# Streaming 640 tokens as 320 and 320 columns instead of 256 and 384 in the weight-stationary products

## The chip, the core and the metric

The kernel runs on one core of a Trainium2 chip. A core has a matrix engine (TensorE; the profile calls its multiplications PE and its weight loads PEld), a vector engine (DVE), a scalar engine (ACT), a general engine (POOL) and a queue that issues transfers (SP). Each has its own instruction stream, and they meet by semaphores. The metric is the device time of one execution in microseconds (us).

## What is computed

Two layers of a transformer step over 640 tokens, 512 latent tokens and 128 context tokens, with a model width of 1024. Everything is float32. A layer is

```python
h = rms_norm(x, norm_attn) * (1.0 + sc_a) + sh_a
proj = h @ w_in                        # 1024 -> 2304: queries, keys, values
...                                    # two kinds of attention
x = x + g_a * (mix @ w_out)            # 1024 -> 1024
h = rms_norm(x, norm_ffn) * (1.0 + sc_f) + sh_f
gate, up = jnp.split(h @ w_gate_up, 2, axis=-1)     # 1024 -> 2 x 2816
x = x + g_f * ((jax.nn.silu(gate) * up) @ w_down)   # 2816 -> 1024
```

Shift, scale and gate (sh, sc, g) come from a conditioning vector, one for the latent and one for the context tokens; the context tokens stand last, in columns 512 to 639.

## The kernel before

The stream x is kept transposed: eight tiles xT[k] of 128 features by 640 tokens. A float32 product is made of three products of rounded halves: each operand is split into a high half (hi) and a low rest (lo), and `prod` adds hi·hi, hi·lo and lo·hi in PSUM. These are the three matmuls of lines 476, 477 and 478.

There are two kinds of product. In the input projection and the attention, the tokens are the stationary operand. In the output projection (`residual` with w_out), the gate and up products (`ffn`) and the down products (`residual` with w_down), the weights are stationary: a block of 128 by 128 weights is loaded and the 640 tokens stream past it. A matmul here streams at most 512 columns, so the tokens go as two groups, and each weight block is loaded once for each group. The groups are `GROUPS`: columns 0 to 255, and 256 to 639. `acc2` hands out the two accumulators as neighbouring slices of one PSUM tile S (three such tiles are in rotation), laid so that the first group ends where one bank ends, and `columns` cuts the operands. For one output block the first group's products all come before the second's: with eight input blocks that is 24 matmuls of 256 columns and then 24 of 384.

The layer's two norms use the same split. The last three output blocks of a `residual` that stands before a norm are done group by group: all three blocks' first group, then the first group's statistics (line 383 sums squares over features on TensorE, lines 95 to 101 take the reciprocal root on DVE, line 387 spreads it over the partitions on TensorE as `rb`), and `norm_apply` writes columns 0 to 255 of the eight normalised tiles hi[k] and lo[k]; then the same for the second group, columns 256 to 639. Per tile `norm_chunk` scales on DVE (line 403), writes hi on ACT (line 86 or 409) and lo on DVE (line 87) or POOL (line 410). In the norm ahead of the gate and up products, the tiles are called k (hi) and q (lo) in the profile.

The order of each engine's instructions is set when the program is built: a scheduler with a timing model of its own sorts ready work, and an engine then runs its list strictly in that order. Waits follow the overlap of columns, tile by tile: a matmul that reads columns 0 to 255 of hi[k] doesn't wait for a write of columns 256 to 639.

Of the kernel before, what the change touches and what calls it, by code (L numbers as in the profile page):

```python
# [21 lines left out]
KC = D // P  # L22
# [3 lines left out]
NT = SEQ + DEC  # L26
# [6 lines left out]
CT = NTILE - 1  # L33
SPLIT = 256
GROUPS = ((0, SPLIT), (SPLIT, NT))
NKEY = DEC + SEQ + PAST
CTX0 = DEC
OLD0 = DEC + SEQ
# [5 lines left out]
class Net:  # L44
# [25 lines left out]
    def mm(self):  # L70
        return self.ps.tile([P, 512], F32, tag="mm", name="mm", bufs=2)

    def acc2(self):

        s = self.S()[:, SPLIT:SPLIT + NT]
        return s, [s[:, a:b] for a, b in GROUPS]


    def split(self, hi, lo, src, bias=None):
# [310 lines left out]
    def norm_apply(self, state, group, rb):  # L390
        g0, g1 = GROUPS[group]
        for k in range(KC):
            self.norm_chunk(state, k, g0, g1, rb)
# [239 lines left out]
    def stack_keys(self, l, pr, d):  # L633

        nc = self.nc
        ka = self.t([P, NKEY], f"k{2 * pr}", F32R)
        kb = self.t([P, NKEY], f"k{2 * pr + 1}", F32R)
        self.ks[pr] = (ka, kb)
# [3 lines left out]
        for i, src in enumerate(tiles):  # L642
            nc.tensor.transpose(ps[:, i * P:(i + 1) * P], src, self.ident)
        src = ps[:, 0:NKEY]
        nc.scalar.activation(ka[0:64], src[0:64], AF.Copy)
# [266 lines left out]


    def columns(self, w, act, group, order):
        a, b = GROUPS[group]
        return [((w[0][:, k], w[1][:, k]), (act[0][k][:, a:b], act[1][k][:, a:b])) for k in order]

    def add_gated(self, l, which, mb, src, a, b):
# [11 lines left out]
    def residual(self, l, act, which, order, nxt=None, side=(), steps=1):  # L930

        if nxt:
            self.stat_begin()
        for mb in range(KC - 3 if nxt else KC):
            w = self.w_next()
            s, parts = self.acc2()
            for i in range(2):  # L940
                self.prod(parts[i], self.columns(w, act, i, order))
            self.add_gated(l, which, mb, s, 0, NT)
            if nxt:
                self.stat_add(mb, 0, NT)
                if mb == 2:
                    self.warm(AF.Silu if nxt[1] else AF.Exp)
            for _ in range(steps):
                self.step(side)
        if not nxt:
            return None  # L950
        while side:
            self.step(side)
        state = self.norm_begin(*nxt)
        last = [(mb, self.w_next(), self.acc2()[1]) for mb in (KC - 3, KC - 2, KC - 1)]
        for i, (a, b) in enumerate(GROUPS):
            for mb, w, parts in last:
                self.prod(parts[i], self.columns(w, act, i, order))
                self.add_gated(l, which, mb, parts[i], a, b)
                self.stat_add(mb, a, b)
            rb = self.mm()  # L960
            self.norm_stats(rb, range(a // P, b // P))
            self.norm_apply(state, i, rb)
        return state[2]

    def ffn(self, l, h, side):
        nc = self.nc
        nxt = None
        for pi, n in enumerate(PARTS):
            if pi == 2:
                while side:  # L970
                    self.step(side)
            if pi < 2:
                act = [[self.t([P, NT], f"{x}{j}", F32R) for j in range(n)] for x in ("hi", "lo")]
            else:
                v = self.t([P, 6, NT], "V", F32R)
                act = [[self.t([P, NT], "Q", F32R, bufs=6) for _ in range(n)], [v[:, j] for j in range(n)]]
            for j in range(n):
                out = []
                for u in range(2):
                    w = self.w_next()  # L980
                    s, parts = self.acc2()
                    for i in range(2):
                        self.prod(parts[i], self.columns(w, h, i, range(KC)))
                    out.append(s)
                    if u == 0:
                        sg = self.t([P, NT], "P", bufs=3)
                        nc.scalar.activation(sg, s, AF.Silu)
                        if pi or j > SKIP:
                            self.step(side)
                nc.vector.tensor_tensor(sg, out[1], sg, ALU.mult)  # L990
                self.split(act[0][j], act[1][j], sg)
                if pi or j > SKIP:
                    self.step(side)
            if pi == len(PARTS) - 1 and l + 1 < DEPTH:
                nxt = (l + 1, 0)
            r = self.residual(l, act, 5, range(n), nxt, side)
        return r
# [92 lines left out]
```

## Time and profile before

| | us |
|---|---|
| median of 3 runs | 1778.3 (1777.71 to 1779.84) |
| the profiled execution | 1776.35 |
| its span, first to last instruction | 1774.6 |
| TensorE busy with matmuls | 1724.7 (97%) |
| DVE busy | 1014.1 (57%) |
| ACT busy | 615.6 (35%) |

The busy time of TensorE counts the pipeline's overlap, so a matmul's own duration there (0.28 us for 256 columns) is longer than the time until the next one starts; the pace is read from the starts. The granted TensorE clock was 0.989 of full speed on average: 1.00 is 2.4 GHz, and in some short stretches it was 0.5, which is 1.2 GHz.

### The profile page before, as it was taken

What the parts mean: (1) busy time and instruction counts of PE and PEld (TensorE: products, weight loads), DVE (VectorE), ACT (ScalarE), POOL (GpSimd) and SP (SyncE); (2) the same over time, 40 slices, a digit from 0 to 9 for tenths busy, and PEclk for the clock granted to TensorE, in tenths of its full rate; (3) what the DMA queues carried; (4) which work ended last, traced back from release to release, by engine and by line L of the source; (5) the groups of instructions that cost most, each with busy time, mean ns of one, the idle gap of its engine ahead of it and who ended that gap; (6) DMA issues with size and microseconds to landing.
All of it is one profiled execution on the core that took longest, in us unless ns stands there. A gap on an engine that the chain in (4) does not pass through costs nothing.

```text
span 1774.6 us, 29153 instructions
## 1 busy us (share of the span) xinstructions
PE 1724.7 (97%) x12194; PEld 1609.7 (91%) x12194; DVE 1014.1 (57%) x1757; ACT 615.6 (35%) x1143; POOL 277.6 (16%) x266
## 2 busy tenths in 40 slices
PE   8889999999999999999999998999999999999999
PEld 6767978888999999899999997888999999999998
DVE  5765667877577877723247885778463232223222
ACT  4422376732422121212235434767252212221220
POOL 0332634400000000000002354453010000000000
PEclk9999999999999999999999999999999999999999
DMA  9343211153155554412222211112212222121212
GB/s 350 109 154 98 55 25 25 49 182 127 56 187 168 162 201 154 145 70 72 77 82 86 81 34 45 31 40 75 72 48 95 72 72 78 66 96 51 93 54 78
DMA packets 44259, 169.20 MB, mean 95 GB/s; under 512 B 5600, under 2 KB 8416, under 8 KB 32864
## 3 DMA queue, kind: packets, MB, share of 16 engines
q1 hardware_dynamic: 44128, 167.34, 28.5%
q8 instruction: 96, 1.57, 0.4%
q14 instruction: 35, 0.29, 0.1%
HBM read 152.90 MB, written 3.93 MB: 88 GB/s over the span
## 4 chain that ended last, share of the span: by engine, by line
PE 91%; DVE 3%; ACT 3%; DMA 1%; issue 1%; POOL 1%; SPq 0%; DVEq 0%; POOLq 0%; ACTq 0%
PE S L476 23%; PE S L477 23%; PE S L478 23%; PE S L687 3%; PE mm L792 3%; PE S L771 2%; PE S L688 2%; PE mm L327 2%; PE mm L788 2%; PE S L233 2%; PE mm L266 1%; PE mm L476 1%; PE mm L477 1%; PE mm L478 1%; DVE mx L707 1%
## 5 line engine op out<-in xcount | busy, mean ns | idle before, releaser
L83 ACT ACTIVATE whi<-raw 128x1024 fp32r<-128x1024 f32 (+2 forms) x192 | 196.2, 1025 | 811.2 <-PE S L477 734.8
L477 PE MATMUL S<-q,whi 128*128 128x256 f32 (+1 forms) x1408 | 436.3, 310 | 0.0
L478 PE MATMUL S<-k,wlo 128*128 128x256 f32 (+1 forms) x1408 | 434.6, 309 | 0.0
L476 PE MATMUL S<-k,whi 128*128 128x256 f32 (+1 forms) x1408 | 432.5, 310 | 1.5 <-ACT k L86 1.4
L84 DVE TENSOR_TENSOR wlo<-raw,whi 128x1024 fp32r<-128x1024 f32 (+2 forms) x192 | 229.9, 1200 | 183.1 <-ACT whi L83 175.9
L476 PEld LDWEIGHTS S<-k,whi 128*128 128x128 f32 x1408 | 265.5, 189 | 12.4 <-issue 10.1
L477 PEld LDWEIGHTS S<-q,whi 128*128 128x128 f32 x1408 | 266.7, 189 | 4.2 <-issue 4.2
L478 PEld LDWEIGHTS S<-k,wlo 128*128 128x128 f32 x1408 | 266.0, 189 | 2.5 <-issue 2.5
L478 PE MATMUL S<-hi,wlo 128*128 128x384 f32 (+1 forms) x768 | 237.9, 310 | 0.0
L477 PE MATMUL S<-lo,whi 128*128 128x384 f32 (+1 forms) x768 | 237.7, 310 | 0.0
L476 PE MATMUL S<-hi,whi 128*128 128x256 f32 (+1 forms) x768 | 237.7, 311 | 0.0
L923 DVE SCALAR_TENSOR_TENSOR x<-S,modT,x 128x128 f32<-128x128 f32 (+2 forms) x137 | 66.4, 524 | 208.6 <-PE S L478 208.6
L310 DVE SCALAR_TENSOR_TENSOR Q<-V,cT,Q 128x512 f32<-128x512 f32 x224 | 152.3, 743 | 0.0
L476 PE MATMUL S<-whi,hi 128*128 128x256 f32 x512 | 147.6, 288 | 1.9 <-ACT Q L241 1.9
L476 PEld LDWEIGHTS S<-hi,whi 128*128 128x128 f32 x768 | 144.0, 188 | 5.9 <-issue 5.0
L478 PEld LDWEIGHTS S<-hi,wlo 128*128 128x128 f32 x768 | 144.5, 188 | 3.4 <-issue 3.4
L478 PE MATMUL S<-whi,lo 128*128 128x256 f32 x512 | 145.8, 286 | 0.0
L477 PE MATMUL S<-wlo,hi 128*128 128x256 f32 x512 | 145.8, 285 | 0.0
L707 DVE TENSOR_REDUCE mx<-S 128x1 f32<-128x768 f32 x128 | 119.1, 950 | 46.3 <-PE S L688 46.0
L477 PEld LDWEIGHTS S<-lo,whi 128*128 128x128 f32 x768 | 144.4, 188 | 0.8 <-issue 0.8
L990 DVE TENSOR_TENSOR P<-S,P 128x640 f32<-128x640 f32 x44 | 36.2, 823 | 148.1 <-PE S L478 148.1
L476 PEld LDWEIGHTS S<-whi,hi 128*128 128x128 f32 x512 | 97.8, 191 | 8.2 <-issue 3.4
(206 smaller groups left out, 2820.7 us busy)
## 6 DMA issues: line engine op xcount, KB each, us to landing
raw<-in_w_gate_up SPq DMA_DIRECT2D x44, 1024.0 KB, 4.8
V<-in_w_mod SPq DMA_DIRECT2D x64, 512.0 KB, 3.9
raw<-in_w_in SPq DMA_DIRECT2D x16, 1024.0 KB, 4.8
raw<-in_w_down SPq DMA_DIRECT2D x16, 1024.0 KB, 5.0
Q<-in_w_mod SPq DMA_DIRECT2D x32, 256.0 KB, 3.1
raw<-in_w_out SPq DMA_DIRECT2D x8, 1024.0 KB, 5.1
raw<-in_w_down SPq DMA_DIRECT2D x8, 768.0 KB, 4.3
raw<-raw SPq DMA_DIRECT2D x40, 128.0 KB, 2.2
```

What stands on the lines that cost most here:

```text
L83: nc.scalar.activation(hi, src, AF.Copy)
L84: nc.vector.tensor_tensor(lo, src, hi.bitcast(F32), ALU.subtract)
L233: nc.tensor.matmul(o, lhsT=l_[k][:, c], rhs=r_[:, w], start=k == 0 and i == 0, stop=k == KC - 1 and i == 2)
L310: ins = nc.vector.scalar_tensor_tensor(a, v, self.cT[:, k, c:c + 1], a, ALU.mult, ALU.add)
L476: self.nc.tensor.matmul(out, lhsT=lh, rhs=rh, start=(i == 0), stop=False)
L477: self.nc.tensor.matmul(out, lhsT=lh, rhs=rl, start=False, stop=False)
L478: self.nc.tensor.matmul(out, lhsT=ll, rhs=rh, start=False, stop=(i == n - 1))
L687: nc.tensor.matmul(out, lhsT=Q[j][:, cols], rhs=keys[:, k0:k0 + n], start=True, stop=False)
L707: nc.vector.tensor_reduce(mx, s[:, 0:n], AX.X, ALU.max, negate=True)
L792: nc.tensor.matmul(o[64 * j:64 * j + 64], lhsT=self.V[:, v, 512 + 64 * j:576 + 64 * j], rhs=pts[j][:, i * P:(i + 1) * P], start=first, sto ...
L923: self.nc.vector.scalar_tensor_tensor(x[:, s:e], src[:, s - a:e - a], self.m(l, which, mb, c), x[:, s:e], ALU.mult, ALU.add)
L990: nc.vector.tensor_tensor(sg, out[1], sg, ALU.mult)
```

## The change

A second pair of groups, `EVEN`, is added: columns 0 to 319, and 320 to 639. `acc2` takes the groups as an argument, with `EVEN` for a default, and `columns` takes the bounds themselves. All gate and up products and the output blocks of the output and down projections use `EVEN`; the last three output blocks of a `residual` that stands before a norm, and the norm itself, stay with `GROUPS`. No instruction is added or removed: each pair of a 256-column and a 384-column matmul becomes two of 320.

```diff
 GROUPS = ((0, SPLIT), (SPLIT, NT))
+EVEN = ((0, NT // 2), (NT // 2, NT))
...
-    def acc2(self):
-
-        s = self.S()[:, SPLIT:SPLIT + NT]
-        return s, [s[:, a:b] for a, b in GROUPS]
+    def acc2(self, groups=EVEN):
+
+        a = 512 - groups[0][1]
+        s = self.S()[:, a:a + NT]
+        return s, [s[:, a:b] for a, b in groups]
...
     def columns(self, w, act, group, order):
-        a, b = GROUPS[group]
+        a, b = group
...
             s, parts = self.acc2()
-            for i in range(2):
-                self.prod(parts[i], self.columns(w, act, i, order))
+            for part, group in zip(parts, EVEN):
+                self.prod(part, self.columns(w, act, group, order))
...
-        last = [(mb, self.w_next(), self.acc2()[1]) for mb in (KC - 3, KC - 2, KC - 1)]
+        last = [(mb, self.w_next(), self.acc2(GROUPS)[1]) for mb in (KC - 3, KC - 2, KC - 1)]
         for i, (a, b) in enumerate(GROUPS):
             for mb, w, parts in last:
-                self.prod(parts[i], self.columns(w, act, i, order))
+                self.prod(parts[i], self.columns(w, act, (a, b), order))
...
                     s, parts = self.acc2()
-                    for i in range(2):
-                        self.prod(parts[i], self.columns(w, h, i, range(KC)))
+                    for part, group in zip(parts, EVEN):
+                        self.prod(part, self.columns(w, h, group, range(KC)))
```

The scheduler, with the same rules, lays TensorE's list out anew. DVE's and ACT's lists differ in a few neighbouring swaps far from any norm; POOL's and SP's are the same. The lines of the changed kernel that follow the two new lines are numbered two higher (476 to 478 become 478 to 480, 383 becomes 385, 387 becomes 389).

On TensorE, where the second layer's output projection ends and its gate products begin (hi_ and lo_ are the attention's output, k_ and q_ the normalised tiles, the low halves wlo and whi the weights), the list before reads

```order
L478 MATMUL S<-hi_10853,wlo 128x384
L387 MATMUL mm<-ident,rstd 128x128 x2
L476 MATMUL S<-k_12972,whi 128x256 x3
L383 MATMUL mm<-ones,PT 128x1 x3
L477 MATMUL S<-q_12980,whi 128x256
L478 MATMUL S<-k_12972,wlo 128x256
L476 MATMUL S<-k_12973,whi 128x256
```

and, some 30 products further, where the second group's reciprocal roots are spread,

```order
L477 MATMUL S<-q_12986,whi 128x256
L478 MATMUL S<-k_12978,wlo 128x256
L476 MATMUL S<-k_12979,whi 128x256
L387 MATMUL mm<-ident,rstd 128x128 x3
L477 MATMUL S<-q_12987,whi 128x256
L478 MATMUL S<-k_12979,wlo 128x256
```

The list of the changed kernel at the same place:

```order
L480 MATMUL S<-hi_10853,wlo 128x384
L389 MATMUL mm<-ident,rstd 128x128 x2
L385 MATMUL mm<-ones,PT 128x1 x3
L389 MATMUL mm<-ident,rstd 128x128 x3
L478 MATMUL S<-k_12972,whi 128x320 x3
L479 MATMUL S<-q_12980,whi 128x320
L480 MATMUL S<-k_12972,wlo 128x320
```

No gate product stands between the two spreads any longer; all of them come behind the second.

The same place of the first layer, on TensorE, before:

```order
L387 MATMUL mm<-ident,rstd 128x128 x2
L383 MATMUL mm<-ones,PT 128x1 x3
L476 MATMUL S<-k_4403,whi 128x256 x3
L477 MATMUL S<-q_4411,whi 128x256
L478 MATMUL S<-k_4403,wlo 128x256
```

and in the changed kernel:

```order
L389 MATMUL mm<-ident,rstd 128x128 x2
L385 MATMUL mm<-ones,PT 128x1 x3
L389 MATMUL mm<-ident,rstd 128x128 x3
L478 MATMUL S<-k_4403,whi 128x320 x3
L479 MATMUL S<-q_4411,whi 128x320
```

Here too the second spread has moved ahead of the first gate product.

## Rows read from the trace of the kernel before

**Rows 1.** The page: engines (busy us, share, instructions), and chain by engine.

```profile
PE 1724.7 (97%) x12194; PEld 1609.7 (91%) x12194; DVE 1014.1 (57%) x1757; ACT 615.6 (35%) x1143; POOL 277.6 (16%) x266
...
PE 91%; DVE 3%; ACT 3%; DMA 1%; issue 1%; POOL 1%; SPq 0%; DVEq 0%; POOLq 0%; ACTq 0%
```

**Rows 2.** Groups by line and shape, TensorE: shapes, count, busy us, mean ns.

```profile
L477 PE MATMUL S<-q,whi 128*128 128x384 f32 x704 | 236.5, 336 | 0.0
...
L478 PE MATMUL S<-hi,wlo 128*128 128x384 f32 x384 | 130.1, 339 | 0.0
...
L478 PE MATMUL S<-Q,wlo 128*128 128x384 f32 x96 | 32.3, 337 | 0.0
```

**Rows 3.** Stretches: length, busy us of each engine, clock, DMA share, GB/s.

```profile
429.00:460.00 31.00, 26.93 (x171) 26.46 (x170) 20.85 (x69) 16.78 (x37) 7.07 (x8) 0.89 0.16 62
1299.00:1328.20 29.20, 26.64 (x163) 25.93 (x161) 19.16 (x53) 16.04 (x37) 7.53 (x8) 0.88 0.17 68
1476.00:1587.50 111.50, 111.50 (x767) 111.50 (x766) 31.43 (x32) 26.64 (x31) 0.00 (x0) 1.00 0.22 76
```

**Rows 4.** Timeline, TensorE in the gate products: start us, us, instruction.

```profile
1503.76 0.28 PE L476 MATMUL S<-k,whi 128*128 128x256 f32 x1
...
1506.59 0.34 PE L476 MATMUL S<-k,whi 128*128 128x384 f32 x1
...
1510.76 0.28 PE L476 MATMUL S<-k,whi 128*128 128x256 f32 x1
```

**Rows 5.** Timeline, TensorE with 512 and with 128 columns.

```profile
49.22 0.39 PE L233 MATMUL S<-whi,hi 128*128 128x512 f32 x1
...
50.62 0.39 PE L233 MATMUL S<-wlo,hi 128*128 128x512 f32 x1
...
257.51 1.50 PE L788 MATMUL mm<-V,wlo 128*128 128x128 f32 x12
```

**Rows 6.** Timeline, TensorE around the second layer's norm before the gate products.

```profile
1299.06 0.60 PE L387 MATMUL mm<-ident,rstd 128*128 128x128 f32 x4
1301.07 0.61 PE L476 MATMUL S<-k,whi 128*128 128x256 f32 x3 [1.41 <-ACT k L86]
1302.83 1.20 PE L383 MATMUL mm<-ones,PT 128*128 128x1 f32 x6 [1.15 <-DVE PT L356]
1303.89 0.56 PE L477 MATMUL S<-q,whi 128*128 128x256 f32 x1
...
1304.46 0.41 PE L476 MATMUL S<-k,whi 128*128 128x256 f32 x1
1304.67 0.41 PE L477 MATMUL S<-q,whi 128*128 128x256 f32 x1
...
1328.17 0.39 PE L476 MATMUL S<-k,whi 128*128 128x256 f32 x1
```

**Rows 7.** Timeline, DVE and POOL at the same place.

```profile
1309.34 0.16 DVE L101 SCALAR_TENSOR_TENSOR rstd<-rs_b,rs_c 128x3 f32<-128x3 f32 x1
1312.23 2.04 DVE L403 SCALAR_TENSOR_TENSOR P<-x,A,mm 128x256 f32<-128x256 f32 x6 [2.74 <-PE mm L387]
1314.19 1.14 DVE L87 SCALAR_TENSOR_TENSOR q<-P,modT,k 128x256 fp32r<-128x256 f32 x3
...
1321.39 1.02 POOL L410 TENSOR_TENSOR q<-P,k 128x384 fp32r<-128x384 f32 x1 [1.18 <-ACT k L409]
```

**Rows 8.** Timeline, TensorE and DVE around the first layer's norm.

```profile
433.96 1.19 PE L387 MATMUL mm<-ident,rstd 128*128 128x128 f32 x4 [4.02 <-DVE rstd L101]
436.27 1.01 PE L476 MATMUL S<-k,whi 128*128 128x256 f32 x3
...
459.72 0.39 PE L476 MATMUL S<-k,whi 128*128 128x256 f32 x1
...
435.19 1.26 DVE L403 SCALAR_TENSOR_TENSOR P<-x,A,mm 128x256 f32<-128x256 f32 x3 [1.38 <-PE mm L387]
...
442.24 0.16 DVE L101 SCALAR_TENSOR_TENSOR rstd<-rs_b,rs_c 128x3 f32<-128x3 f32 x1
```

## The prediction

> **What bounds the kernel now.** I read the page first: TensorE is busy for 97% of the span, and 91% of the chain that ended last is its own work [rows 1]. DVE and ACT are far from full. So two questions decide: at what pace the products stream, and where TensorE stands still. The stretches come next [rows 3]. In the gate products of the second layer TensorE is busy for all of 111.50 us at full clock, with DVE at 31 us and ACT at 27 us: nobody else matters there. Around each norm ahead of the gate products it isn't full: 26.93 of 31.00 us and 26.64 of 29.20 us, at a mean clock of 0.89 and 0.88. With the two levels of 1.00 and 0.50 that is some 7 us at half clock in each. The timeline then gives the paces and the waits.
>
> **The pace, and what the new split gains.** A matmul's price in a full stream is the time from its start to the next one's. In one gate product, 24 matmuls of 256 columns take 1506.59 - 1503.76 = 2.83 us, 117.9 ns each, and the 24 of 384 columns behind them 4.17 us, 173.8 ns each [rows 4]. A pair costs 291.7 ns. The trace has no 320 columns, so I bound their price by the neighbours. Six steps of 512 columns take 50.62 - 49.22 = 1.40 us, 233 ns each; twelve passes of 128 columns take 1.50 us, some 110 ns from start to start once the last one's tail of 0.28 us is off [rows 5]. Per column that is 0.86 ns at 128, 0.461 at 256, 0.453 at 384 and 0.456 at 512. From 384 on the price is proportional; at 128 it is a floor of another kind, by the look of it the weight load; and 256 stands near that floor and pays some 2 ns over proportion.
> - A straight line through 256 and 384 gives 320 columns 145.8 ns: two cost 291.7, and nothing is gained.
> - In proportion to 384 they take 144.8 ns: a pair gains 2.1 ns.
> - The line through 384 and 512, drawn back, gives 143.9 ns: 3.9 ns.
>
> I take the middle one: 320 is farther from the floor than 256, and 384 and 512 agree on proportion.
>
> How many pairs change: 704 on each of the three lines in the gate and up products, 384 and 96 in the `residual` calls [rows 2], so 3 x 1184 = 3552. Exempt are the last three output blocks ahead of the three norms that a `residual` feeds: 2 x 3 x 8 input blocks of the output projection and 3 x 6 of the first layer's last down product, 66 x 3 = 198. That leaves 3354. The first three gate and up products of each layer are costed apart below, 72 pairs each; 3210 remain. The gain is 3210 x 2.1 ns = 6.7 us, with ends of 0 and 12.5 us. All of it is on the path, as these stretches are TensorE's own. Evictions read the same 640 columns of S in as many instructions, and the pool's three tiles turn as before, so I cost that at nothing: DVE and ACT are idle for over two thirds of that stretch [rows 3].
>
> The Trainium skill speaks against any gain here. TensorE: Matmul & The Clock Gate, section "Back-to-back issue gap", gives a warm matmul N/2.4 + 2.5 ns: a fixed part for each instruction and a part in proportion to its columns. By that rule any two-way split of 640 columns costs the same, and the change would give nothing; the paces here are longer than its 109 and 162 ns, so it can't be taken as it stands, but its shape is that of the first of the three bounds.
>
> **What the change takes away at the norm.** The exempted blocks and the norm keep 256 and 384, but the gate product behind them doesn't. Its first group now reads columns 0 to 319, and 256 to 319 are written by the norm's second group. In the order before, three gate and up products run on the first group's columns, 72 matmuls of 256, while the second group's statistics, roots and scaling go on. In the changed order the second spread (387, now 389) stands ahead of all gate products, and TensorE, which takes its list in order, has nothing in between.
>
> I time this from DVE, whose list around the norm is unchanged. In the second layer:
> - DVE finishes the second group's roots at 1309.34 + 0.16 = 1309.50 [rows 7]. Before, TensorE came to the spread late, out of the middle of the products, and DVE waited 2.74 us for it. Now TensorE is already waiting, at half clock. The first group's spread of two tiles took 1.23 us at half clock, from its start at 433.96 to DVE's first scaling at 435.19 [rows 8]. A third tile adds two passes of about 0.21 us, the half-clock pace [rows 6]; with 0.14 us for the signal, scaling starts at 1311.3, some 0.9 us earlier than the 1312.23 of before.
> - The first low half was ready about 2.4 us after scaling began, when the first of the three instructions of 1314.19 ended [rows 7]. So TensorE gets three matmuls in and then runs on from 1313.7.
> - The three products are 144 matmuls of 320; 141 of them at 144.8 ns take 20.4 us: 1334.1 at full clock. The norm's pace doesn't hold it: the last low half came at 1321.39 + 1.02 = 1322.41 [rows 7], now near 1321.5, and over half of these matmuls come behind it.
> - Before, this work was done at 1328.17, when the fourth product begins [rows 6]. The loss is 5.9 us.
>
> In the first layer the roots end at 442.40; scaling starts at 444.2, the run at 446.6, and the three products end at 467.0 against 459.72 [rows 8]: 7.3 us. Here the early spread wins nothing, since before TensorE was punctual. Together 13.2 us.
>
> The clock comes on top. Before, some 7 us at half clock lay around each norm [rows 3], and TensorE resumed in them: in the second layer it starts on the low halves at 1303.89, and still goes at 0.21 us a matmul at 1304.46 [rows 6]. Now the pause before the first full run is longer, from the end of the output projection at 1299.06 to 1313.7 with a few short instructions in it. I expect half clock for 3 to 6 us behind the restart, which loses half of that; the bounds for each norm are 0 (the clock rises in the pause) and 3.5 us (the 7 us of before, all on products). I take 2.3 us each, 4.6 together. What the clock cost before is inside the times 1328.17 and 459.72 already.
>
> **The sum.** +13.2 + 4.6 - 6.7 = +11.1 us on the profiled execution's 1776.35, so 1787.5; the median stands 1.95 us above that execution, which puts the forecast at 1789.4 us. The ends are +13.2 + 0 - 12.5 = +0.7 (1779.0) and +13.2 + 7.0 - 0 = +20.2 (1798.5). About 0.2%, 3.6 us, is what a measurement of this kernel can tell from no change.
>
> **The rivals.**
> - *No gain in the stream.* If the per-matmul part is fixed, 320 columns cost 145.8 ns, and only the norm's loss is left: +17.8 us, 1796.1. The pace at 512, in line with 384 and without a visible fixed part, speaks against it; that only one size stands between the floor and 384 speaks for it. 20%.
> - *Faster.* The stream gains more than the norms lose. It decides at 17.8 us / 3210 = 5.5 ns a pair, that is when a matmul of 320 columns takes under 143.1 ns. At 142.0 ns the pairs would gain 7.7 ns, 24.7 us, and the time would be 1771.4. For it: at 2.4 GHz a column a cycle would be 133 ns, so there is room. Against it: no size in the trace goes under 0.453 ns a column. 4%.
> - *The cover isn't lost.* The pause costs nothing, because the second group is normalised while the first's tail still runs; then only the gain stays: 1771.6. The order speaks against it, since the second group's statistics need the last output block, and no work stands between it and the second spread. 2%.
> - *A draw.* The clock recovers inside the pause and the stream gains its upper bound: +0.7 to +3.6 us, about 1780. 6%.
>
> The forecast keeps 68%. Slower: 0.68 + 0.20 = 0.88; same 0.06; faster 0.06. The range of 1783 to 1798 takes in the forecast's own spread and the no-gain case and leaves out the draw's lower part, the faster cases and the outer tails.
>
> **What would show it.** In the new profile, from start to start: 320 columns at 144 to 146 ns in the second layer's gate products. At both norms: no gate product between the two spreads, a pause until two to three us after DVE begins to scale columns 256 on, then a run that starts at half clock. From the end of the output projection to the fourth gate or up product some 38 us in place of 29.1 in the second layer, and 9 to 10 us more in the first. The input projection's norm, whose readers take tokens in tiles of 128, shows no difference. The prediction is wrong if 320 columns stream in under 143 ns, or if TensorE finds gate work during the second group's norm.

## The result, and the profile after

The changed kernel takes 1802.92 us (median of four runs, 1800.99 to 1805.54) against 1778.01 us (median of four): a ratio of 1.0145, with a 95% interval of 1.0125 to 1.0165. The forecast was 1789.4 us, in a range of 1783 to 1798: the sign was right, the size less than half of what came, and the time lies above the range. The profiled execution took 1805.54 us.

The page after, engines and chain, as [rows 1] of before:

```profile
PE 1738.5 (96%) x12194; PEld 1623.2 (90%) x12194; DVE 1015.8 (56%) x1757; ACT 615.6 (34%) x1143; POOL 277.4 (15%) x266
...
PE 90%; DVE 4%; ACT 2%; DMA 2%; issue 1%; POOL 1%; SPq 0%; DVEq 0%; POOLq 0%; ACTq 0%
```

TensorE is busy for 13.8 us longer with as many instructions, and the span grew by 29.2 us (1803.8 from 1774.6). So the time went to two places: TensorE stands still for longer, and it works for longer. The stretches answer to [rows 3]: the two norms ahead of the gate products, and the second layer's second part of the gate products.

```profile
431.60:470.80 39.20, 27.45 (x165) 26.61 (x164) 23.91 (x72) 18.23 (x38) 7.01 (x8) 0.78 0.13 50
1317.10:1354.00 36.90, 26.31 (x157) 25.40 (x156) 22.51 (x56) 17.73 (x38) 7.49 (x8) 0.81 0.14 53
1503.10:1616.20 113.10, 113.10 (x769) 113.10 (x768) 31.46 (x32) 26.66 (x31) 0.00 (x0) 1.00 0.21 75
```

At the norms TensorE has as much work as before, but the stretches are 39 and 37 us long in place of 31 and 29, at a mean clock of 0.78 and 0.81 in place of 0.89 and 0.88. In the third line TensorE is full at full clock, as before, and takes longer.

The second norm in the timeline of TensorE, as [rows 6]:

```profile
1316.97 0.34 PE L480 MATMUL S<-hi,wlo 128*128 128x384 f32 x1
1317.15 0.61 PE L389 MATMUL mm<-ident,rstd 128*128 128x128 f32 x4
1321.01 0.80 PE L385 MATMUL mm<-ones,PT 128*128 128x1 f32 x6 [3.26 <-DVE PT L358]
1327.71 1.62 PE L389 MATMUL mm<-ident,rstd 128*128 128x128 f32 x6 [5.90 <-DVE rstd L103]
1330.52 1.17 PE L478 MATMUL S<-k,whi 128*128 128x320 f32 x3 [1.20 <-ACT k L88]
1331.94 0.63 PE L479 MATMUL S<-q,whi 128*128 128x320 f32 x1 [0.24 <-DVE q L89]
...
1335.57 0.47 PE L480 MATMUL S<-k,wlo 128*128 128x320 f32 x1
1335.83 0.47 PE L479 MATMUL S<-q,whi 128*128 128x320 f32 x1
...
1354.74 0.31 PE L478 MATMUL S<-k,whi 128*128 128x320 f32 x1
```

No gate product stands between the two spreads. TensorE waits for DVE's roots (5.90 us), then for the first tile that ACT writes (1.20 us), runs on at half clock (0.26 us from 1335.57 to 1335.83), and begins the fourth product at 1354.74. From the start of the last output-projection matmul, the first line, that is 37.8 us; before it was 29.3. DVE's side, as [rows 7], shows the links:

```profile
1327.40 0.16 DVE L103 SCALAR_TENSOR_TENSOR rstd<-rs_b,rs_c 128x3 f32<-128x3 f32 x1
1329.45 2.04 DVE L405 SCALAR_TENSOR_TENSOR P<-x,A,mm 128x256 f32<-128x256 f32 x6 [1.89 <-PE mm L389]
1331.40 0.74 DVE L89 SCALAR_TENSOR_TENSOR q<-P,modT,k 128x256 fp32r<-128x256 f32 x2
```

The first norm, as [rows 8], on TensorE:

```profile
431.51 0.34 PE L480 MATMUL S<-hi,wlo 128*128 128x384 f32 x1
...
445.20 1.62 PE L389 MATMUL mm<-ident,rstd 128*128 128x128 f32 x6 [6.28 <-DVE rstd L103]
448.02 1.17 PE L478 MATMUL S<-k,whi 128*128 128x320 f32 x3 [1.19 <-ACT k L88]
449.43 0.63 PE L479 MATMUL S<-q,whi 128*128 128x320 f32 x1 [0.25 <-DVE q L89]
...
471.54 0.31 PE L478 MATMUL S<-k,whi 128*128 128x320 f32 x1
```

From the last output-projection matmul, the first line, to the fourth product this takes 40.0 us. Before, the last output-projection matmuls of the two layers were

```profile
428.83 0.34 PE L478 MATMUL S<-hi,wlo 128*128 128x384 f32 x1
...
1298.88 0.34 PE L478 MATMUL S<-hi,wlo 128*128 128x384 f32 x1
```

and with the fourth products at 459.72 [rows 8] and 1328.17 [rows 6] that was 30.9 and 29.3 us. The two norms cost 9.1 and 8.5 us more, 17.6 together.

The stream is read where TensorE does nothing but stream: from the first down matmul of the second layer to the first gate matmul behind it (192 pairs), and on to the next down matmul (384 pairs). After:

```profile
1446.78 0.31 PE L478 MATMUL S<-hi,whi 128*128 128x320 f32 x1
...
1503.10 0.31 PE L478 MATMUL S<-k,whi 128*128 128x320 f32 x1
...
1616.37 0.31 PE L478 MATMUL S<-hi,whi 128*128 128x320 f32 x1
```

The same three starts before:

```profile
1419.18 0.28 PE L476 MATMUL S<-hi,whi 128*128 128x256 f32 x1
...
1475.79 0.28 PE L476 MATMUL S<-k,whi 128*128 128x256 f32 x1
...
1587.68 0.28 PE L476 MATMUL S<-hi,whi 128*128 128x256 f32 x1
```

The gate part went from 111.89 to 113.27 us: a pair from 291.4 to 295.0 ns, 3.6 dearer. The down part went from 56.61 to 56.32: a pair from 294.8 to 293.3 ns, 1.5 cheaper. Of the 3210 pairs away from the norms, 704 x 3 - 144 = 1968 are gate and up products and 1242 the others. So the stream cost 1968 x 3.6 - 1242 x 1.5 ns, some 5 us, where a gain of 6.7 was forecast. Of the 29.2 us between the two profiled executions, 17.6 and 5 are accounted for; the rest lies in stretches whose instructions the change leaves alone, such as the second layer's attention (308.0 us in place of 303.9), and single executions of the kernel before differ by nearly as much (1774 to 1780).

### The profile page after: what moved, and what is told of

It reads as the page before. It is cut to its first block, busy times and chain, and to the rows that moved or that the text cites. A ratio compares the mean times of both kernels' runs of the same rounds, so it can differ in the third digit from the quotient of the medians.

```text
span 1803.8 us, 29150 instructions
## 1 busy us (share of the span) xinstructions
PE 1738.5 (96%) x12194; PEld 1623.2 (90%) x12194; DVE 1015.8 (56%) x1757; ACT 615.6 (34%) x1143; POOL 277.4 (15%) x266
## 4 chain that ended last, share of the span: by engine, by line
PE 90%; DVE 4%; ACT 2%; DMA 2%; issue 1%; POOL 1%; SPq 0%; DVEq 0%; POOLq 0%; ACTq 0%
PE S L479 23%; PE S L480 23%; PE S L478 23%; PE S L689 3%; PE mm L794 3%; PE S L773 3%; PE S L690 2%; PE mm L329 2%; PE mm L790 2%; PE S L235 2%; PE mm L268 1%; PE mm L478 1%; PE mm L479 1%; PE mm L480 1%; DVE mx L709 1%; DVE P L405 1%
## 5 line engine op out<-in xcount | busy, mean ns | idle before, releaser
L479 PE MATMUL S<-q,whi 128*128 128x320 f32 x1408 | 440.7, 313 | 0.5 <-DVE q L89 0.5
L478 PE MATMUL S<-k,whi 128*128 128x320 f32 x1408 | 434.9, 311 | 2.4 <-ACT k L88 2.4
L480 PE MATMUL S<-k,wlo 128*128 128x320 f32 x1408 | 436.3, 310 | 0.0
L478 PE MATMUL S<-hi,whi 128*128 128x320 f32 (+2 forms) x768 | 238.0, 310 | 0.0
L480 PE MATMUL S<-hi,wlo 128*128 128x320 f32 (+2 forms) x768 | 237.7, 310 | 0.0
L479 PE MATMUL S<-lo,whi 128*128 128x320 f32 (+2 forms) x768 | 237.3, 310 | 0.0
```

The costliest lines, as they stand in the source:

```text
L478: self.nc.tensor.matmul(out, lhsT=lh, rhs=rh, start=(i == 0), stop=False)
L479: self.nc.tensor.matmul(out, lhsT=lh, rhs=rl, start=False, stop=False)
L480: self.nc.tensor.matmul(out, lhsT=ll, rhs=rh, start=False, stop=(i == n - 1))
```

## The experiments

The theory after the new trace: the loss is the norm's cover (the gate products that TensorE had to do during the second group's norm), some 17 us, and a stream that is dearer in the gate products. Each run is a ratio to the kernel before, with its 95% interval, run on the same chip. Lines that an edit adds move the line numbers of the profile by as many.

**The cover kept.** Only the first three gate and up products of a layer go back to the old cut:

```diff
+                    cut = GROUPS if pi == 0 and 2 * j + u < 3 else EVEN
-                    s, parts = self.acc2()
-                    for part, group in zip(parts, EVEN):
+                    s, parts = self.acc2(cut)
+                    for part, group in zip(parts, cut):
```

> The change with one exception more: the first three gate and up products of each layer keep 256 and 384, so that the first group's columns can again be worked on during the second group's norm. Theory (the loss is two things: the lost cover at the two norms, some 17 us, and a stream of 320 columns that in the gate and up products is 3.6 ns a pair dearer and in the other products 1.5 ns a pair cheaper): the norms go back to the times of before, and 1968 pairs x 3.6 ns - 1210 pairs x 1.5 ns = +5 us remain, about 1783 us. Rival A (the stream gains the 6.7 us that were forecast, and the norms cost more than thought): 1771 us. Rival B (the norm's cover is not what was lost): about 1800 us, as the changed kernel.

Measured: 1783.44 us, 1.0037 (1.0025 to 1.0050). The second norm in its timeline is that of before again:

```profile
1304.95 0.61 PE L389 MATMUL mm<-ident,rstd 128*128 128x128 f32 x4
1306.96 0.61 PE L478 MATMUL S<-k,whi 128*128 128x256 f32 x3 [1.41 <-ACT k L88]
1308.73 0.83 PE L385 MATMUL mm<-ones,PT 128*128 128x1 f32 x6 [1.15 <-DVE PT L358]
1309.60 0.38 PE L479 MATMUL S<-q,whi 128*128 128x256 f32 x1
```

Three products give back most of the loss, and the stream's loss of some 6 us stays. Both rivals fall.

**The cover taken away alone.** The kernel before, with the cut of those three products two columns further, which moves two columns from one matmul to the next and makes the first group wait for the norm's second (as an edit of the changed kernel):

```diff
-EVEN = ((0, NT // 2), (NT // 2, NT))
+EVEN = GROUPS
+PAST2 = ((0, SPLIT + 2), (SPLIT + 2, NT))
...
+                    cut = PAST2 if pi == 0 and 2 * j + u < 3 else EVEN
```

> The kernel before with the cover alone taken away: all groups are 256 and 384, but in the first three gate and up products of each layer the cut stands at column 258 in place of 256, so that the first group reads two columns that the norm's second group writes. The stream costs the same. Theory: both norms lose what the changed kernel lost there, 8.4 to 8.7 us each: +17 us, 1795 us, with half clock for 4 to 6 us behind each restart. Rival (the widths, not the columns waited for, make the norm slower): 1778 us.

Measured: 1795.77 us, 1.0104 (1.0089 to 1.0119), 18.5 us. The waits of TensorE from 1310 us on:

```profile
PE mm L390 <- DVE rstd L104: 5.6, 1, 5.6
PE mm L386 <- DVE PT L359: 3.3, 1, 3.3
PE S L479 <- ACT k L89: 1.2, 1, 1.2
```

These are the changed kernel's waits (5.90, 3.26 and 1.20 us above) with hardly a column moved, so it is the two columns waited for, not the widths. The two runs add up: 18.5 and 6.6 us are 25.1, and the change lost 24.9.

**The residual products alone.** The gate products keep `GROUPS`; the output and down projections take `EVEN`.

> The new cut in the output and down projections alone; all gate and up products keep 256 and 384. Theory: 1210 pairs x -1.5 ns = -1.8 us, about 1776 us, with 320 columns at 146.7 ns in these products. Rival (what these products gained in the changed kernel's trace was chance): 1778 us, no difference.

Measured: 1776.68 us, 0.9994 (0.9985 to 1.0003). From start to start 320 columns took 146.7 ns there, as expected; the 1.8 us are too few to be told from nothing.

**Another cut.** `EVEN` at column 288, the cover kept.

> As the run with the cover kept, but the new cut stands at column 288: 288 and 352 columns. It gives two more points of the price by width. If the price follows the width alone and 320 lies on a step, 288 and 352 fall on either side of it: 288 in line with 256 at 0.460 ns a column, 132.5 ns, and 352 in line with 384 at 0.452, 159 ns, a pair of 291.5 ns. If any cut other than 256 is dearer (by where the second group's columns begin), the pair costs 294 to 295 ns, as two of 320 do in the gate and up products.

One execution: 1779.64 us. In the gate products 132.1 ns for 288 columns and 160.6 for 352, a pair of 292.7; in the down and output projections 133.4 and 160.2, 293.6. So 288 came out as the line says, 352 above it. Neither statement held: the pair lies between 291.5 and 295. And each width has two prices, one for each kind of product, which is no law of width. The two kinds stream different tiles. The second group also begins elsewhere: 288 columns are 1152 bytes, 128 off a multiple of 256, where 256 and 320 columns are multiples, and the runs below show that such a step can count. So 352 was priced in another place than 384 and 320.

**All tiles 32 bytes further,** with the cut of the cover-kept run, and then with the kernel before.

```diff
+        nc.vector.memset(self.t([P, 8], "pad"), 0.0)
         cond = self.t([P, KC, 2], "cond")
```

> The run with the cover kept, and one tile of 32 bytes a partition allocated ahead of nearly all others, so that every token and weight tile lies 32 bytes further; nothing else moves. So far one width has had different prices in products that stream different tiles (384 columns: 173.5 ns in the gate products, 175.9 in the others). Theory (where a tile lies sets part of a matmul's price): the mean price of 320 columns moves by over 0.5 ns a matmul in at least one group of products, 4000 matmuls x 0.5 ns = 2 us or more in all, either way. Rival (the price goes by width and kind of product, whatever the place): 147.4 and 146.7 ns again to within 0.2, and 1783 us.

> The kernel before with the same 32 bytes ahead of its tiles. Theory of the place: 256 and 384 columns leave 118.0 and 173.5 ns by over 0.5 ns too, and the time moves by 2 us or more in either direction. Rival: the same prices, 1777 us.

Measured: 1784.16 us, 1.0040 (1.0027 to 1.0053), and 1778.36 us, 1.0001 (0.9992 to 1.0010). The prices came back to 0.1 ns: 147.4 and 146.7 ns for 320 columns, 118.0 and 173.5 in the gate products of before. A shift of all tiles by 32 bytes doesn't count; no larger one was tried.

**The weights further than the tokens.** The tile stands between the token tiles and the weight tiles now. What is allocated behind the weights moves with them, the low halves of the gate products' tokens too:

```diff
+            if k == 0:
+                nc.vector.memset(self.t([P, 32], "pad"), 0.0)
             if k % 2 == 0:
                 wh = self.t([P, 2, 512], "whi", F32R, bufs=4)
```

> The run with the cover kept, with 128 bytes allocated between the token tiles and the weight tiles: the weights and the low halves of the gate products' tokens lie 128 bytes further, their high halves and all tokens of the other products lie where they were. Theory (the price depends on how the weights' place stands to the tokens'): the gate products leave 147.4 ns or the others 146.7 ns by over 0.5 ns. Rival (only the place within some 64 bytes, or nothing, counts): the same two prices.

One execution: 1780.25 us. The three starts of the second layer:

```profile
1422.27 0.30 PE L480 MATMUL S<-hi,whi 128*128 128x320 f32 x1
...
1478.59 0.31 PE L480 MATMUL S<-k,whi 128*128 128x320 f32 x1
...
1590.79 0.30 PE L480 MATMUL S<-hi,whi 128*128 128x320 f32 x1
```

The gate part takes 112.20 us in place of 113.27, 146.1 ns a matmul in place of 147.5: the same matmuls, with 128 bytes put between two tiles. The down part stays at 56.32. In the last down products of each layer, whose tokens lie in other tiles, 320 columns went the other way, from 145.1 to 148.7 ns.

**The same with the kernel before,** at 64, 128, 256 and 384 bytes.

> The kernel before, its groups 256 and 384 unchanged, with 64 bytes allocated between the token tiles and the weight tiles. The last run showed that the price of a matmul goes by where the weights lie to the streaming tokens. Theory: the prices of 256 and 384 columns move here as well, by 0.5 to 2 ns, differently in the gate products (118.0 and 173.5 ns) and the others (118.8 and 175.9); with about 7000 such matmuls the time moves by 3 to 10 us one way or the other, while the two norms' pauses stay. Rival: 320 columns alone are sensitive, and this kernel stays at 1777 us with the same prices.

> The same with 128 bytes. Theory: the prices of the run with 128 bytes and 320 columns recur where the widths are the same: 384 columns at 173.9 ns in the down and output products and 174.2 in the gate products, 256 at 119.9 and 118.3. That is a pair 0.8 ns cheaper in the first and 1.0 dearer in the second: 2112 x 1.0 - 1152 x 0.8 = +1 us, 1778 us. Rival: 1777 us with the prices of before.

> The same with 256 bytes. If the place counts by its remainder to some small power of two (up to 256 bytes), this run's prices are those of the kernel before, 118.0 and 173.5 ns in the gate products, to within 0.2. If it counts by a larger one, they differ by over 0.5 ns somewhere.

> The same with 384 bytes, the most that fits. If the place counts by its remainder to 256 bytes or less, its prices are those of the run with 128 bytes; else another set.

Measured: 0.9974 (0.9959 to 0.9989), 0.9996 (0.9986 to 1.0006), 1.0004 (0.9994 to 1.0014) and 1.0004 (0.9994 to 1.0013). The three starts with 256 bytes:

```profile
1420.19 0.28 PE L478 MATMUL S<-hi,whi 128*128 128x256 f32 x1
...
1476.80 0.28 PE L478 MATMUL S<-k,whi 128*128 128x256 f32 x1
...
1588.69 0.28 PE L478 MATMUL S<-hi,whi 128*128 128x256 f32 x1
```

56.61 and 111.89 us, those of no shift to the last digit. The run with 384 bytes repeats the one with 128 as exactly: 117.7 and 174.1 ns in the gate products, 119.5 and 173.7 in the others. So the distance of the weights to the tokens counts by its remainder to 256 bytes, as far as steps of 64 show. With 64 bytes,

```profile
1419.05 0.28 PE L478 MATMUL S<-hi,whi 128*128 128x256 f32 x1
...
1474.95 0.28 PE L478 MATMUL S<-k,whi 128*128 128x256 f32 x1
...
1587.06 0.28 PE L478 MATMUL S<-hi,whi 128*128 128x256 f32 x1
```

the down part takes 55.90 us and the gate part 112.11, and 256 columns where the tokens are stationary go from 119.0 to 114.8 ns. The expected time there, 3 to 10 us either way, came as 4.6 less; its ten executions are spread from 1767.3 to 1778.6 us, wider than any other kernel's here, and no run shows why.

**The stream in the other places.** Three more runs: the cover-kept cut and the residual cut at 64 bytes, and the kernel before at 192.

> The run with the cover kept, 320 columns elsewhere, with the weights 64 bytes further. It shows what the change's stream is worth where the weights lie best so far. Theory (the step that failed in the forecast is the price of 320, which goes by place; in a good place it is in proportion, 0.4518 ns a column): 144.6 to 145.5 ns, a pair of 290 ns against 292.0 and 291.2 for 256 and 384 in this place, so that it is 3 to 6 us faster than the kernel before with 64 bytes (0.9974 of the kernel before): 0.995 to 0.997, about 1770 us. Rival (320 columns are dear in every place): 147 ns and 1.000 or above.

> The kernel before with the weights 192 bytes further, the one remainder to 256 bytes in steps of 64 not yet seen. Theory: a fourth set of prices within 115 to 120 ns for 256 and 173.4 to 176 ns for 384 columns; the time within 0.3% of the kernel before. Rival (prices depend on the distance's sign only, so that 192 is like 64): the prices of the run with 64 bytes, 114.8 ns for 256 columns where the tokens are stationary.

> The new cut in the output and down projections alone, with the weights 64 bytes further. If 320 columns take 145 ns there, a pair costs 290 ns against 291.2 at 256 and 384 in the same place: 1200 pairs x 1.2 ns = 1.5 us below the kernel before with 64 bytes, 0.9965 of the kernel before. Rival: 320 at 146.7 ns there too, 293.3 ns a pair, and 0.999.

Measured: 1771.56 us, 0.9963 (0.9950 to 0.9975); 1771.13 us, 0.9961 (0.9948 to 0.9973); 1775.41 us, 0.9983 (0.9974 to 0.9992). The three starts of the first:

```profile
1413.89 0.31 PE L480 MATMUL S<-hi,whi 128*128 128x320 f32 x1
...
1470.22 0.32 PE L480 MATMUL S<-k,whi 128*128 128x320 f32 x1
...
1581.82 0.31 PE L480 MATMUL S<-hi,whi 128*128 128x320 f32 x1
```

The gate part takes 111.60 us, 145.3 ns a matmul: a pair of 290.6 ns, below the 292.0 of 256 and 384 columns in the same place and below the 291.4 of before. The rival, dear in every place, falls for the gate products. It holds for the down part: 56.32 us in each of the three places tried, 146.7 ns, where 256 and 384 got down to 55.90. At 192 bytes:

```profile
1415.96 0.28 PE L478 MATMUL S<-hi,whi 128*128 128x256 f32 x1
...
1471.02 0.28 PE L478 MATMUL S<-k,whi 128*128 128x256 f32 x1
...
1583.37 0.28 PE L478 MATMUL S<-hi,whi 128*128 128x256 f32 x1
```

The down part falls to 55.06 us, a pair of 286.8 ns, the lowest of all; 256 columns take 113.8 ns there, below the span that was expected, and the time fell by 0.4% where 0.3% was the most expected; the gate part rises to 112.35. The rival, that the sign of the distance counts, falls: where the tokens are stationary, 256 columns took 117.5 ns, not 114.8. These two kernels, the cover-kept cut with 64 bytes and the kernel before with 192, are the best seen: 0.4% faster than the kernel before, and not told apart by their intervals. The residual cut at 64 bytes beats the kernel before by 0.2% and adds nothing to the same place without it: its 320 columns stay at 146.7 ns, as its rival said.

The second layer's parts side by side, the first down part and the gate part behind it, in us:

| groups | weights moved by | down, 192 pairs | gate and up, 384 pairs |
|---|---|---|---|
| 256, 384 | 0 | 56.61 | 111.89 |
| 256, 384 | 64 | 55.90 | 112.11 |
| 256, 384 | 128 | 56.28 | 112.01 |
| 256, 384 | 192 | 55.06 | 112.35 |
| 256, 384 | 256 | 56.61 | 111.89 |
| 320, 320 | 0 | 56.32 | 113.27 |
| 320, 320 | 64 | 56.32 | 111.60 |
| 320, 320 | 128 | 56.32 | 112.20 |

Is it the distance, or the weights' own place? The mean price of 384 columns in the kernel before, from start to start at full clock, in ns, by the tokens that stream:

| weights moved by | output and down | last down of a layer | gate and up |
|---|---|---|---|
| 0 | 175.9 | 173.9 | 173.5 |
| 64 | 173.4 | 173.4 | 173.6 |
| 128 | 173.7 | 175.6 | 174.1 |
| 192 | 173.4 | 173.7 | 175.2 |

A place of the weights that is dear with one set of tokens is cheap with another, so the weights' own place alone doesn't set the price. By the addresses that the built program gives its tiles, the dear case is in each column the one in which the weights lie 128 bytes, by remainder to 256, from the high halves of the tokens (unmoved, the weights have remainder 224, the high halves 96, 224 and 32). The other two widths show no such single rule: 320 columns kept 146.7 ns in the products of the first column, in all three places tried.

## Why the prediction was right in sign and wrong in size

- **The bound.** TensorE's own stream and its pauses at the norms were the right places to look; both moved the time, and the runs that take each alone add up to the whole.
- **The norms: right.** 17.8 us were forecast, 17.6 read from the traces, 18.5 measured by the run that takes the cover alone. The pieces agree too. From the end of the roots to the first scaling 1.80 us were worked out, 1329.45 - 1327.56 = 1.89 came; from there to the first low half's instruction 1331.40 - 1329.45 = 1.95, and 1.96 before. "Some 38 us in place of 29.1" in the second layer came as 37.8 and 29.3; "9 to 10 us more" in the first as 9.1. TensorE went at half clock from 1330.52 to about 1336.1 in the second layer and for 4.2 us behind the restart in the first, inside the 3 to 6 us expected. In part the sum was lucky: from the run's restart to the fourth product 22.7 us were forecast in the second layer (20.4 of matmuls, 2.3 for the clock), and 1354.74 - 1331.94 = 22.80 came, but as some 20.8 of dearer matmuls (141 at 147.4 ns) and 2.0 for the clock; in the first layer, at 22.1, the clock took only some 1.3.
- **The stream: wrong, and this is the step that failed.** "I take the middle one: 320 is farther from the floor than 256, and 384 and 512 agree on proportion." In the gate products 320 columns took 147.4 ns, above even the upper of the three bounds (145.8), and a pair lost 3.6 ns in place of gaining 2.1. All three bounds took the price for a function of the width, read off one place each: the 384 from the gate products, the 512 from the projection at the start, where the tokens are stationary and the weights stream, each with its own tiles. The trace before held the warning, as 384 columns took 173.5 ns in the gate products and 175.9 in the down products. Even [rows 2] hint at it, with mean durations of 336 and 339 ns for the same 384 columns, and I passed over them. The runs with the weights moved showed what the price also goes by, and with 64 bytes the gate products' 320 columns took 145.3 ns, inside the bounds. (The lowest bound has a slip as well: with 1.40 / 6 us for 512 columns the line gives 144.0 ns, not 143.9, and an upper end of 11.9 us, not 12.5. Nothing that failed hangs on it.)
- **The sum.** 17.8 - 6.7 = 11.1 was forecast; 18.5 + 6.6 = 25.1 is what the two parts measured alone, and the change 24.9. The no-gain rival, at 17.8, was nearer than the forecast, for another reason than it gave.
- **The Trainium skill's rule.** TensorE: Matmul & The Clock Gate, "Back-to-back issue gap", gives a price by columns plus a fixed part, for a matmul by itself; the prediction took it for a stream, where it would make the split indifferent. Here a pair of the same 640 columns took from 286.8 to 295.0 ns at full clock, by split and by place; the measurement decides.

What stays open is the mechanism: whether the weight load and the stream contend for something, and for what. The runs show a period of 256 bytes in the distance and that a common shift by 32 bytes changes nothing; why 320 columns are dear in the gate products' first place and cheap with 64 bytes they do not. In the output and down products the distances of the high and of the low halves to the weights moved together, and in the gate products the high halves' alone, so that of the low halves wasn't tried by itself.

## What to carry to other kernels

A cut that is shared between a producer's two halves and its consumer is a handover: move it on one side by two columns, and the consumer waits for the other half (18.5 us here, in two places, with the same work). When a regular stream is full at full clock, a price per instruction need not be a function of its shape alone; before changing shapes, compare the price of one shape in different products, and if it differs, try moving the operands' places first, since that takes some bytes of SBUF and no work on TensorE.

## What was not expected of the hardware

- A matmul's price depends on the distance in SBUF between the weights and the streaming tokens, by its remainder to 256 bytes: 256 columns took 113.8 to 119.5 ns in the down and output projections (without the last down products of a layer), 384 took 173.4 to 175.9, at full clock, and moving all tiles together by 32 bytes left the prices of the products with stationary weights within 0.1 ns.
